# Squares on ScalarE, x loaded twice, a later weight schedule and turned PSUM banks in a hybrid decoder block

## The chip, the core and the metric

The kernel runs on one core of a Trainium2 chip. The metric is the device time of one execution in microseconds (us), the median over several runs; lower is better. Profiles are taken in one extra execution by the hardware profiler. TensorE appears there as PE (matmul) and PEld (weight load), VectorE as DVE, ScalarE as ACT, GpSimd as POOL, SyncE as SP; a name with q (SPq, ACTq) is the engine's instruction queue, on which DMAs are issued.

## The reference, cut to what matters

One decoder layer, 1024 tokens of width 1024, float32. x is normalised per token and modulated per channel, then multiplied by one wide input matrix:

```python
mod = c @ w_ada + b_ada
shift, scale, gate = jnp.split(mod, 3, axis=-1)
h = rmsnorm(x, norm_g) * (1.0 + scale) + shift      # mean of x*x over the 1024 channels of a token
proj = h @ w_in                                      # 1024 -> 6656 columns
q, k, v, g_attn, xr, g_rnn, m_attn, m_rnn = jnp.split(proj, SPLIT_POINTS, axis=-1)
q, k = partial_rope(q, positions), partial_rope(k, positions)
y_attn = sliding_window_attention_with_sinks(q, k, v, sinks) * silu(g_attn)
xr = causal_depthwise_conv(xr, conv_w, conv_b)
y_rnn = rg_lru(xr, ...) * silu(g_rnn)
merged = sigmoid(m_attn) * (y_attn @ w_attn_proj) + sigmoid(m_rnn) * (y_rnn @ w_rnn_proj)
out = rmsnorm(x + gate * (merged @ w_out), final_g)
```

## The kernel before, in words

All of h is kept transposed: channels on the 128 partitions, the 1024 tokens along the row, in eight tiles (kc = 0 to 7), each cut into two halves of 512 tokens (hf). Float32 accuracy is reached with two numbers of a shorter type for each factor: a high part (`hh`, `wh`, a copy into float32r on ACT) and the rest (`hl`, `wl`, a subtraction on DVE). Every product is three matmuls: high x high, rest x high, high x rest. The order of instructions on every engine is written out by hand (`manual_schedule`), so each engine runs its list strictly in the order of the program.

**The start.** SP asks for the eight tiles `xT` of x transposed, 512 KB each, first; then for the modulation weights `wada` (two tiles of 512.5 KB for each kc, by `load_ss`, six buffers) and for the first weights of `w_main` (256 KB halves, by `load_half`, six buffers `r`). `c_row` and `pk` (per-channel constants) are asked for on ACT's queue, `posr` and `invf` (for the rope angles) on POOL's. DVE works out the rope angles (`angles`, some 30 small instructions, up to L321). ACT squares each `xT` tile (L254), in four buffers; DVE adds pairs of squares (L256); TensorE sums over the channels with a column of ones, 8 groups of 128 tokens for each of the five sums (L250, `sums`), into PSUM bank `bk[2]`. DVE adds the five groups (L339), ACT takes the root (`root_of`), DVE the reciprocal, and TensorE spreads it over the partitions (L348, `spread`) into `bk[0]` and `bk[1]`. `modulate(kc, a)` is a DVE multiply-and-sum over a `wada` tile and a broadcast copy of c (`c_bc`, L237); it gives shift and scale of the 128 channels of kc. `norm` multiplies by the spread root (L353, L356), `high` makes `hh` on ACT straight from the normalised tile (L359), `affine` makes the full h in place on ACT (L363), `low` subtracts (L368).

Four column groups of 128 of `w_main` are multiplied while h is being made (`starts`, L170 by `mm_k`): for each kc 24 matmuls of 128x512. `starts[0]` and `starts[1]` (k) add up in `pmain` tiles, `starts[2]` (q, first part) in `bk[2:]`, `starts[3]` (q, second part) in `bk[:2]`. `cast_w`/`rest_w` split their weights: half 0 serves kc 0 to 3 and lies in four tiles `first`; half 1 serves kc 4 to 7 and lies in the five-buffer tags `wh`/`wl` (`slot()`).

**After the start.** TensorE goes on with the v product (`v_product`, L1383 to L1385, 96 matmuls for each half of the tokens), two products of the merge gate (`merge`, L170, 48 matmuls each), one small matmul into `bk[0]` (L1437), and then 22 pairs of column groups by a Strassen-like scheme (`Pair`, `run`, L597), seven products each. `place` gives pair i its banks: `b1 = bk[0]`, `b2 = bk[1 + par]`, `b3 = bk[3]` and, for one product at the very end, `bk[2 - par]`; par alternates from pair to pair. In the meantime DVE and ACT rotate q and k (`rope_a` with rotation, `rope_b` without), form the differences of h that the scheme needs (`differences`, `make_operands`) and split weights. Near the end of the pairs the attention is woven in: `open_attn` asks for its first tiles, `scores` is L1140, `values` L1212. Behind the last pair the products `rp` of the recurrent branch (L170, two PSUM tiles `rp0` and `rp1`, which take the places of `bk[0]`, `bk[1]` and of `bk[2]`, `bk[3]`) run between the attention's units. The last pair ends with two readings of its banks: `keep` (L646, ACT, copies `b2`) and `add` (L668, DVE, adds the fourth bank).

The line that chooses the banks:

```python
p.place(7 * i, i % 2, i == len(pairs) - 1, ...)
```

Of the kernel before, what the change touches and what calls it, by code (L numbers as in the profile page):

```python
# [22 lines left out]
P = 128  # L23
S = 1024
# [27 lines left out]
def tile_hybrid_block(ctx, tc, x, x_t, pk, rows, posr, posi, invf, c_row, w_ss, w_gate, w_main, w_v,  # L52
# [4 lines left out]
    def dma(dst, src, eng=nc.sync):  # L57
        dst, src = (a.bitcast(F32) if a.dtype == F32R else a for a in (dst, src))
        return eng.dma_start(dst, src)  # L59
# [96 lines left out]
    hx = h_ctx.enter_context(tc.tile_pool(name="hx", bufs=8))  # L156
    acc, r_bc = (hx.tile([P, S], F32, tag="X", name=n_) for n_ in ("acc", "r_bc"))
    xT = [xx.tile([P, S], F32, name=f"xT{kc}") if kc % 4 == 3 else
# [27 lines left out]
    with ExitStack() as st:  # L186
        sp = st.enter_context(tc.tile_pool(name="start", bufs=1, side="right"))
        first = [tuple(sp.tile([P, HALF], F32R, name=f"{n}0{i}") for n in ("wh", "wl"))
                 for i in range(4)]
        sqs = [acc, sp.tile([P, S], F32, name="sqa"), r_bc, sp.tile([P, S], F32, name="sqb")]  # L190
        c_row_t = sqs[3][0:1, :]
        posr_t = sp.tile([P, 64], I32, name="posr_t")
        invf_t = sp.tile([P, 1], F32, name="invf_t")
        dma(c_row_t, c_row, A)
        dma(pk_t[:], pk, A)
        dma(posr_t[:], posr, G)
        dma(invf_t[:], invf, G)

        wada, halfw = {}, {}

        def load_ss(kc):
            for a in range(2):
                wa_t = sp.tile([P, D + 1], F32, tag="wada", name="wada", bufs=6)
                dma(wa_t[:], w_ss[a * D + kc * P:a * D + (kc + 1) * P, :])
                wada[kc, a] = wa_t
# [3 lines left out]

        for kc in range(KC):  # L210
            dma(xT[kc][:], x_t[kc * P:(kc + 1) * P, :])
        load_ss(0)
        for i in range(4):
            load_wh(i, 0)
        load_ss(1)
        load_ss(2)
        for i in range(2):
            load_wh(i, 1)

        make_identity(nc, ident)  # L220
        one = sp.tile([P, P], F32, name="one")
        V.memset(one[:], 1.0)
        root = sp.tile([P, 1], F32, name="root")
        A.activation(root[:], one[:, 0:1], AF.Sqrt)
        c_bc = sp.tile([P, D + 1], F32, name="c_bc")
        V.memset(c_bc[:, D:], 1.0)
        for hf in range(2):
            T.matmul(bk[hf], one[0:1, :], c_row_t[:, SL[hf]], start=True, stop=True)
        for hf in range(2):
            A.copy(c_bc[:, SL[hf]], bk[hf])  # L230

        mods = sp.tile([P, 16], F32, name="mods")
        gsc = sp.tile([P, 8], F32, name="gsc")

# [12 lines left out]

        def sums(i, kc, js=range(8)):
            for j in js:
                T.matmul(bk[2][:, 8 * i + j:8 * i + j + 1], sqs[kc % 4][:, j * P:(j + 1) * P],  # L250
                         one[:, 0:1], start=True, stop=True)

        def square(kc):
            A.activation(sqs[kc % 4][:], xT[kc][:], AF.Square)  # L254
            if kc < 6 and kc % 2:
                V.tensor_tensor(out=sqs[kc % 4 - 1][:], in0=sqs[kc % 4 - 1][:],  # L256
                                in1=sqs[kc % 4][:], op=ALU.add)
                sums(kc // 2, kc - 1)

        trn = sp.tile([P, 2, 64], F32, name="trn")  # L260
        trf = trn[:].rearrange("p a t -> p (a t)")
# [60 lines left out]

        csn = sp.tile([P, 3, 64], F32, name="csn")

        def table():
# [7 lines left out]

        rr = tiny("rr", 8)
        groups = bk[2][:, 0:40].rearrange("p (g j) -> p j g", j=8)

        def root_of(hf):
            r1 = rr[:, 4 * hf:4 * hf + 4]
            V.tensor_reduce(out=r1, in_=groups[:, 4 * hf:4 * hf + 4, :], axis=AX.X, op=ALU.add)  # L339
            V.tensor_scalar(out=r1, in0=r1, scalar1=1.0 / D, scalar2=EPS, op0=ALU.mult,  # L340
                            op1=ALU.add)
            A.activation(r1, r1, AF.Sqrt)
# [30 lines left out]
        def cast_w(i, h):  # L373
            W0[i, h] = slot() if h else first[i]
            cast(W0[i, h], halfw[i, h], 0.125 if i > 1 else 1.0)
# [7 lines left out]

        angles()
        square(0)
        square(1)
        for kc in range(2, 6):
            square(kc)
        square(6)
        sums(3, 6)  # L390
        square(7)
        for hf in range(2):
            sums(4, 7, range(4 * hf, 4 * hf + 4))
        modulate(0, 0)
        root_of(0)
        root_of(1)
        spread(0)
        spread(1)
        cast_w(0, 0)
        cast_w(1, 0)  # L400
        modulate(0, 1)
        norm(0, 0)
        high(0, 0)
        rest_w(0, 0)
        norm(0, 1)
        high(0, 1)
# [16 lines left out]
        load_ss(3)  # L423
        for i in (2, 3):
            load_wh(i, 1)
        for kc in range(1, KC):
            norm(kc)
            for hf in range(2):
                high(kc, hf)
            affine(kc)  # L430
            if kc == 1:
                table()
            if kc + 1 < KC:
                for a in range(2):
                    modulate(kc + 1, a)
            if kc in (2, 3):
                for i in (0, 1) if kc == 2 else (2, 3):
                    cast_w(i, 1)
                    rest_w(i, 1)
            low(kc)  # L440
            if kc + 3 < KC:
                load_ss(kc + 3)
            if kc == 3:
                rv = [load_half(w_v[i // 2][:, SL[i % 2]]) for i in range(4)]
            if kc < 3:
                for terms in ("h", "l"):
# [990 lines left out]
    T.matmul(bk[0], hh[0][0][:, 0:P], hh[0][0], start=True, stop=True)  # L1437
# [45 lines left out]
    for u in range(32 + 3):  # L1483
# [286 lines left out]
```

## Time and profile before

| what | value |
|---|---|
| median of 3 runs | 961.26 us (961.08 to 964.26) |
| profiled execution: its time, its span | 960.87 us, 959.2 us |
| granted TensorE clock, mean over the span | 0.991 |
| PE busy | 924.6 us (96%) |
| DVE busy | 684.2 us (71%) |
| ACT busy | 535.1 us (56%) |
| bytes moved | 164.21 MB |

Rows of the order of time (the timeline) give start, duration, engine, line, operation, written tile, read tiles, and in brackets how long the engine had been idle before and what ended that. The view of waits gives total, number of times and the longest. The view of windows gives for each stretch of time the busy time of each engine, then the granted clock, the mean share of the DMA engines and GB/s. Lines are those of the kernel before unless the text says otherwise.

### The profile page before, as it was taken

What the parts mean: (1) busy time and instruction counts of PE and PEld (TensorE: products, weight loads), DVE (VectorE), ACT (ScalarE), POOL (GpSimd) and SP (SyncE); (2) the same over time, 40 slices, a digit from 0 to 9 for tenths busy, and PEclk for the clock granted to TensorE, in tenths of its full rate; (3) what the DMA queues carried; (4) which work ended last, traced back from release to release, by engine and by line L of the source; (5) the groups of instructions that cost most, each with busy time, mean ns of one, the idle gap of its engine ahead of it and who ended that gap; (6) DMA issues with size and microseconds to landing.
All of it is one profiled execution on the core that took longest, in us unless ns stands there. A gap on an engine that the chain in (4) does not pass through costs nothing.

```text
span 959.2 us, 12443 instructions
## 1 busy us (share of the span) xinstructions
PE 924.6 (96%) x4305; PEld 769.6 (80%) x4305; DVE 684.2 (71%) x1044; ACT 535.1 (56%) x1019; POOL 86.5 (9%) x148
## 2 busy tenths in 40 slices
PE   4989999999999999999999998899999999999997
PEld 3867988888788888888887887778888888888886
DVE  4596688889866984888498474869899846657422
ACT  3355365654565954885678783868888632222211
POOL 0011000000000000000000001334444400000000
PEclk9999999999999999999999999989999999999999
DMA  9462355967232443336045257969566266446311
GB/s 355 131 218 80 102 184 186 315 222 253 72 111 96 139 154 99 110 110 207 35 165 173 91 175 244 307 240 296 177 198 224 83 238 245 161 147 241 132 66 66
DMA packets 80916, 164.21 MB, mean 171 GB/s; under 512 B 12531, under 2 KB 28915, under 8 KB 80854
## 3 DMA queue, kind: packets, MB, share of 16 engines
q1 hardware_dynamic: 77300, 155.24, 47.7%
q0 software_dynamic: 2256, 6.03, 1.9%
q10 hardware_dynamic: 1298, 2.15, 0.6%
q8 instruction: 34, 0.56, 0.2%
q14 instruction: 28, 0.23, 0.1%
HBM read 114.01 MB, written 49.78 MB: 171 GB/s over the span
## 4 chain that ended last, share of the span: by engine, by line
PE 90%; DVE 4%; DMA 2%; ACT 2%; issue 1%; POOL 0%; SPq 0%; DVEq 0%; ACTq 0%; POOLq 0%
PE bk L597 41%; PE rp L170 14%; PE pmain L170 6%; PE rp L1633 5%; PE pgate L891 5%; PE pmain L1633 4%; PE bk L170 4%; PE s_ps L1140 3%; PE pv L1212 3%; PE bk L250 2%; PE pt L1178 1%; DMA qs<-q_d 1%; PE bk L1383 1%; PE bk L1384 1%; PE bk L1385 1%
## 5 line engine op out<-in xcount | busy, mean ns | idle before, releaser
L597 PE MATMUL bk<-nh,wl 128*128 128x512 f32 x352 | 138.0, 392 | 0.4 <-DVE wl L107 0.4
L597 PE MATMUL bk<-nh,wh 128*128 128x512 f32 x352 | 137.8, 392 | 0.0
L597 PE MATMUL bk<-nl,wh 128*128 128x512 f32 x352 | 137.6, 391 | 0.0
L107 DVE TENSOR_TENSOR wl<-r,wh 128x512 fp32r<-128x512 f32 x109 | 79.3, 732 | 24.1 <-ACT wh L101 24.1
L101 ACT CAST wh<-r 128x512 fp32r<-128x512 f32 x109 | 66.9, 618 | 46.1 <-PE bk L1385 12.7
L597 PEld LDWEIGHTS bk<-nh,wl 128*128 128x128 f32 x352 | 66.5, 189 | 15.2 <-DVE wl L107 1.4
L597 PEld LDWEIGHTS bk<-nh,wh 128*128 128x128 f32 x352 | 66.4, 189 | 13.9
L597 PEld LDWEIGHTS bk<-nl,wh 128*128 128x128 f32 x352 | 66.5, 189 | 13.7
L597 PE MATMUL bk<-hh,wh 128*128 128x512 f32 x176 | 68.6, 390 | 0.0
L597 PE MATMUL bk<-hh,wl 128*128 128x512 f32 x176 | 68.6, 390 | 0.0
L597 PE MATMUL bk<-hl,wh 128*128 128x512 f32 x176 | 68.5, 389 | 0.0
L107 DVE TENSOR_TENSOR wl<-ws,wh 128x512 fp32r<-128x512 f32 x76 | 51.8, 686 | 0.5 <-ACT wh L101 0.5
L1164 ACT ACTIVATE p<-p,small 128x129 f32<-128x129 f32 x128 | 50.1, 401 | 0.0
L101 ACT CAST wh<-ws 128x512 fp32r<-128x512 f32 x76 | 45.8, 614 | 2.3 <-DVE ws L619 1.1
L59 POOL DMA_DIRECT2D yh_d<-yh x1 | 0.6, 557 | 491.7 <-ACT yh L958 491.7
L1140 PE MATMUL s_ps<-ks,qs 128*128 128x256 f32 (+1 forms) x256 | 37.6, 289 | 3.2 <-DMA qs<-q_d 3.2
L597 PEld LDWEIGHTS bk<-hh,wh 128*128 128x128 f32 x176 | 33.0, 188 | 7.7 <-ACT wh L101 0.9
L1650 ACT ACTIVATE o<-xo 128x1024 f32<-128x1024 f32 (+2 forms) x10 | 8.9, 889 | 53.4 <-DVE xo L1649 53.4
L597 PEld LDWEIGHTS bk<-hl,wh 128*128 128x128 f32 x176 | 33.0, 188 | 6.9
L597 PEld LDWEIGHTS bk<-hh,wl 128*128 128x128 f32 x176 | 33.0, 188 | 6.7
L1140 PEld LDWEIGHTS s_ps<-ks,qs 128*128 128x128 f32 x256 | 32.4, 190 | 3.9 <-issue 3.6
L700 ACT ACTIVATE c<-bk 128x512 f32<-128x512 f32 x29 | 17.3, 597 | 31.0 <-PE bk L597 31.0
(361 smaller groups left out, 2327.0 us busy)
## 6 DMA issues: line engine op xcount, KB each, us to landing
r<-w_main SPq DMA_DIRECT2D x100, 256.0 KB, 4.1
wada<-w_ss SPq DMA_DIRECT2D x16, 512.5 KB, 4.8
qs<-q_d SPq DMA_DIRECT2D x16, 512.0 KB, 5.4
ks<-k_d SPq DMA_DIRECT2D x24, 192.0 KB, 3.5
xT<-x_t SPq DMA_DIRECT2D x8, 512.0 KB, 7.3
q_d<-rhi SPq DMA_DIRECT2D x16, 256.0 KB, 4.2
q_d<-rlo SPq DMA_DIRECT2D x16, 256.0 KB, 3.8
sma_d<-c SPq DMA_DIRECT2D x16, 256.0 KB, 2.8
```

What stands on the lines that cost most here:

```text
L101: A.copy(dst[0][:], src)
L107: V.tensor_tensor(out=dst[1][:], in0=src, in1=f32(dst[0][:]), op=ALU.subtract)
L170: mm = T.matmul(ps[hf], ww, xx[kc][hf], start=(kc == 0 and ww is w_h and xx is xh), stop=(kc == KC - 1 and xx is xl))
L250: T.matmul(bk[2][:, 8 * i + j:8 * i + j + 1], sqs[kc % 4][:, j * P:(j + 1) * P], one[:, 0:1], start=True, stop=True)
L597: W["pe"] = T.matmul(ps, ww[:, c], b[kc][xx_], start=(first and kc == 0 and i == 0), stop=(kc == 3 and i == 2), skip_group_check=not first)
L700: A.activation(t["t"], s(), AF.Tanh, scale=0.5)
L891: W["pe"] = T.matmul(ps[:, SL[hf]], ww[:, c0:c0 + P], xx_[:, SL[hf]], start=(ic == 0 and i == 0), stop=(ic == 1 and i == 2))
L1140: W["pe"] = T.matmul(o, qs[:, j, qc], ks[:, b, k0 + (0 if n else P):k0 + 256], start=(b == 0), stop=(b == 1))
L1164: A.activation(px[:, j, :], px[:, j, :], AF.Exp, bias=sm[:, 0, j:j + 1], accum_out=sm[:, 1, j:j + 1])
L1178: W["pe"] = T.transpose(pt[:, j, :], px[:, j, 0:P], ident[:])
L1212: W["pe"] = T.matmul(pv[:], b, m[:].rearrange("p j q -> p (j q)"), start=(i == 0), stop=(i == len(prods) - 1))
L1633: T.matmul(ps[:, sl], lhs[k][th][:, ts_], w[:, sl], start=(k == 0 and w is h_ and lhs is mh), stop=(k == KC - 1 and lhs is ml))
```

## The change

The sum of squares is now taken along token rows: x is loaded a second time, untransposed (eight tiles of 128 tokens), before everything else on SP's queue, and ACT squares each tile with a running sum (`accum_out`), giving eight columns of `rr`; TensorE's sums, DVE's additions and the four square buffers are gone. `mean` and `root_of` work on four columns at a time. The row tiles share the `wada` buffers, now seven; one of them lies in a tile `xlast`. `xT[kc]` is asked for behind the `wada` tiles of its kc. `posr` and `invf` move to ACT's queue, the copies of `c_bc` from ACT to DVE. In the loop over kc the affine tile comes first and `hh` is a plain copy of it. Half 0 of the start's weights now lies in `slot()`, half 1 in `first`; the v weights are split during kc = 5, 6 and 7 instead of behind the loop. The last four kc of the loop take the starts in the order 2, 3, 0, 1. ACT copies `starts[2]` out of its banks (`kept`) before the v product, which now begins in `bk[2:]`; the banks of `merge` are exchanged likewise, and `place` starts with the other parity. `open_attn` asks for the first k and q tiles ahead of the sinks. The tiles `nh` are laid out in another order, and the pool of the start is released tile by tile.

```diff
-    acc, r_bc = (hx.tile([P, S], F32, tag="X", name=n_) for n_ in ("acc", "r_bc"))
+    r_bc, xlast = (hx.tile([P, S], F32, tag="X", name=n_) for n_ in ("r_bc", "xlast"))
...
-        sp = st.enter_context(tc.tile_pool(name="start", bufs=1, side="right"))
+        sp = pool(st, "start", side="right")
...
+        c_row_t = r_bc[0:1, :]
         dma(c_row_t, c_row, A)
+        dma(posr_t[:], posr, A)
+        dma(invf_t[:], invf, A)
         dma(pk_t[:], pk, A)
-        dma(posr_t[:], posr, G)
-        dma(invf_t[:], invf, G)
...
-                wa_t = sp.tile([P, D + 1], F32, tag="wada", name="wada", bufs=6)
+                wa_t = sp.tile([P, D + 1], F32, tag="wada", name="wada", bufs=7)
...
-        for kc in range(KC):
+        def load_xt(kc):
             dma(xT[kc][:], x_t[kc * P:(kc + 1) * P, :])
-        load_ss(0)
-        for i in range(4):
-            load_wh(i, 0)
-        load_ss(1)
-        load_ss(2)
-        for i in range(2):
-            load_wh(i, 1)
+
+        def load_x0(i):
+            t = xlast if i == 6 else sp.tile([P, D + 1], F32, tag="wada", name="xt", bufs=7)
+            dma(t[:, :D], x[i * P:(i + 1) * P, :])
+            xt.append(t[:, :D])
+
+        for i in range(8):
+            load_x0(i)
...
-        for hf in range(2):
-            A.copy(c_bc[:, SL[hf]], bk[hf])
...
-        def sums(i, kc, js=range(8)):
-            for j in js:
-                T.matmul(bk[2][:, 8 * i + j:8 * i + j + 1], sqs[kc % 4][:, j * P:(j + 1) * P],
-                         one[:, 0:1], start=True, stop=True)
-
-        def square(kc):
-            A.activation(sqs[kc % 4][:], xT[kc][:], AF.Square)
-            if kc < 6 and kc % 2:
-                V.tensor_tensor(out=sqs[kc % 4 - 1][:], in0=sqs[kc % 4 - 1][:],
-                                in1=sqs[kc % 4][:], op=ALU.add)
-                sums(kc // 2, kc - 1)
+        def square(i):
+            junk = sp.tile([P, D], BF16, tag="junk", name="junk")
+            A.activation(junk[:], xt[i], AF.Square, accum_out=rr[:, i:i + 1])
...
-            W0[i, h] = slot() if h else first[i]
+            W0[i, h] = first[i] if h else slot()
...
         angles()
-        square(0)
-        square(1)
-        for kc in range(2, 6):
-            square(kc)
-        square(6)
-        sums(3, 6)
+        for hf in range(2):
+            V.tensor_copy(c_bc[:, SL[hf]], bk[hf])
+        for i in range(7):
+            square(i)
+            if i == 1:
+                load_ss(0)
+                load_xt(0)
+                for j in range(4):
+                    load_wh(j, 0)
+            if i == 3:
+                load_ss(1)
+                load_xt(1)
+        mean(0)
+        root_of(0)
         square(7)
-        for hf in range(2):
-            sums(4, 7, range(4 * hf, 4 * hf + 4))
+        load_ss(2)
+        load_xt(2)
+        for i in range(2):
+            load_wh(i, 1)
+        spread(0)
         modulate(0, 0)
-        root_of(0)
+        mean(1)
         root_of(1)
-        spread(0)
-        spread(1)
+        A.copy(r_bc[:, SL[0]], bk[0])
+        modulate(0, 1)
         cast_w(0, 0)
-        cast_w(1, 0)
-        modulate(0, 1)
         norm(0, 0)
         high(0, 0)
+        spread(1)
         rest_w(0, 0)
+        cast_w(1, 0)
         norm(0, 1)
         high(0, 1)
         rest_w(1, 0)
+        cast_w(2, 0)
+        A.copy(r_bc[:, SL[1]], bk[1])
+        rest_w(2, 0)
         affine(0)
-        modulate(1, 0)
-        cast_w(2, 0)
+        cast_w(3, 0)
         low(0)
-        for hf in range(2):
-            A.copy(r_bc[:, SL[hf]], bk[hf])
-        cast_w(3, 0)
-        rest_w(2, 0)
-        modulate(1, 1)
         rest_w(3, 0)
+        for a in range(2):
+            modulate(1, a)
...
             norm(kc)
+            affine(kc)
             for hf in range(2):
-                high(kc, hf)
-            affine(kc)
+                A.copy(hh[kc][hf], xT[kc][:, SL[hf]])
...
-                for i in (3, 2, 0, 1):
+                for i in (2, 3, 0, 1):
...
-        wv = [split(slot(), r) for r in rv]
+            if kc in (5, 6, 7):
+                for i in ((0,), (1,), (2, 3))[kc - 5]:
+                    wv.append(split(slot(), rv[i]))
...
-    nh = [hn.tile([P, S], F32R, name=f"nh{i}") for i in range(KC)]
+    nh = dict((i, hn.tile([P, S], F32R, name=f"nh{i}")) for i in (3, 7, 2, 6, 1, 5, 0, 4))
...
-            p.place(7 * i, i % 2, i == len(pairs) - 1,
+            p.place(7 * i, (i + len(pairs) + 1) % 2, i == len(pairs) - 1,
...
+        fill_sink = sink(0)
+        load_kq(0)
         dma(W["sink"][:], rows[0:1, 2048:2048 + NH].to_broadcast([P, NH]))
-        sink(0)
-        load_kq(0)
+        fill_sink()
...
+    kept = [blk(), blk()]
+    for hf in range(2):
+        A.copy(kept[hf], starts[2][1][hf])
     now(*[rope_b(lambda hf=hf: starts[3][1][hf], hf, q_d[0]) for hf in range(2)])
-    now(*[rope_a(lambda hf=hf: starts[2][1][hf], hf, q_d[0]) for hf in range(2)])
-    v_product(bk[:2], 0)
+    v_product(bk[2:], 0)
+    for hf in range(2):
+        now(rope_a(lambda: kept[hf], hf, q_d[0]))
...
-    v_product(bk[2:], 1)
-    v_store(bk[:2], 0)
+    v_product(bk[:2], 1)
+    v_store(bk[2:], 0)
...
-    merge(0, bk[:2])
-    v_store(bk[2:], 1)
+    merge(0, bk[2:])
+    v_store(bk[:2], 1)
...
-    merge_out(0, bk[:2])
+    merge_out(0, bk[2:])
...
-    merge(1, bk[2:])
-    merge_out(1, bk[2:])
+    merge(1, bk[:2])
+    merge_out(1, bk[:2])
     T.matmul(bk[0], hh[0][0][:, 0:P], hh[0][0], start=True, stop=True)
```

More of the change, by code (lines that the diff above doesn't have):

```diff
@@ L38 @@
 PAD_R = 480
+PAD_S = 544
 def _split_const(u):
@@ L186, in tile_hybrid_block @@
     with ExitStack() as st:
-        sp = st.enter_context(tc.tile_pool(name="start", bufs=1, side="right"))
+        sp = pool(st, "start", side="right")
         first = [tuple(sp.tile([P, HALF], F32R, name=f"{n}0{i}") for n in ("wh", "wl"))
                  for i in range(4)]
-        sqs = [acc, sp.tile([P, S], F32, name="sqa"), r_bc, sp.tile([P, S], F32, name="sqb")]
-        c_row_t = sqs[3][0:1, :]
+        one = sp.tile([P, P], F32, name="one")
+        c_bc = sp.tile([P, D + 1], F32, name="c_bc")
+        trn = sp.tile([P, 2, 64], F32, name="trn")
+        csn = sp.tile([P, 3, 64], F32, name="csn")
         posr_t = sp.tile([P, 64], I32, name="posr_t")
         invf_t = sp.tile([P, 1], F32, name="invf_t")
+        mods = sp.tile([P, 16], F32, name="mods")
+        gsc = sp.tile([P, 8], F32, name="gsc")
+        root = sp.tile([P, 1], F32, name="root")
+        rr = sp.tile([P, 8], F32, name="rr")
+        sp.tile([P, PAD_S // 4], F32, name="pad_s")
+        c_row_t = r_bc[0:1, :]
         dma(c_row_t, c_row, A)
+        dma(posr_t[:], posr, A)
+        dma(invf_t[:], invf, A)
         dma(pk_t[:], pk, A)
-        dma(posr_t[:], posr, G)
-        dma(invf_t[:], invf, G)
-        wada, halfw = {}, {}
+        xt, wada, halfw = [], {}, {}
         def load_ss(kc):
             for a in range(2):
-                wa_t = sp.tile([P, D + 1], F32, tag="wada", name="wada", bufs=6)
+                wa_t = sp.tile([P, D + 1], F32, tag="wada", name="wada", bufs=7)
                 dma(wa_t[:], w_ss[a * D + kc * P:a * D + (kc + 1) * P, :])
@@ L208, in load_wh @@
             halfw[i, h] = load_half(w_main[i][:, SL[h]])
-        for kc in range(KC):
+        def load_xt(kc):
             dma(xT[kc][:], x_t[kc * P:(kc + 1) * P, :])
-        load_ss(0)
-        for i in range(4):
-            load_wh(i, 0)
-        load_ss(1)
-        load_ss(2)
-        for i in range(2):
-            load_wh(i, 1)
+        def load_x0(i):
[4 more added lines that the diff above has]
+            load_x0(i)
         make_identity(nc, ident)
-        one = sp.tile([P, P], F32, name="one")
         V.memset(one[:], 1.0)
-        root = sp.tile([P, 1], F32, name="root")
         A.activation(root[:], one[:, 0:1], AF.Sqrt)
-        c_bc = sp.tile([P, D + 1], F32, name="c_bc")
         V.memset(c_bc[:, D:], 1.0)
@@ L228, in tile_hybrid_block @@
             T.matmul(bk[hf], one[0:1, :], c_row_t[:, SL[hf]], start=True, stop=True)
-        for hf in range(2):
-            A.copy(c_bc[:, SL[hf]], bk[hf])
-        mods = sp.tile([P, 16], F32, name="mods")
-        gsc = sp.tile([P, 8], F32, name="gsc")
         def modulate(kc, a):
@@ L246, in tiny @@
             return sp.tile([P, n], F32, name=name)
-        def sums(i, kc, js=range(8)):
-            for j in js:
-                T.matmul(bk[2][:, 8 * i + j:8 * i + j + 1], sqs[kc % 4][:, j * P:(j + 1) * P],
-                         one[:, 0:1], start=True, stop=True)
-        def square(kc):
-            A.activation(sqs[kc % 4][:], xT[kc][:], AF.Square)
-            if kc < 6 and kc % 2:
-                V.tensor_tensor(out=sqs[kc % 4 - 1][:], in0=sqs[kc % 4 - 1][:],
-                                in1=sqs[kc % 4][:], op=ALU.add)
-                sums(kc // 2, kc - 1)
-        trn = sp.tile([P, 2, 64], F32, name="trn")
+        def square(i):
+            junk = sp.tile([P, D], BF16, tag="junk", name="junk")
+            A.activation(junk[:], xt[i], AF.Square, accum_out=rr[:, i:i + 1])
         trf = trn[:].rearrange("p a t -> p (a t)")
@@ L321, in angles @@
             V.tensor_scalar(out=trf, in0=trf, scalar1=-3.1415925, scalar2=None, op0=ALU.max)
-        csn = sp.tile([P, 3, 64], F32, name="csn")
         def table():
@@ L332, in table, with mean @@
             dma(cs4_d, cs_d.unsqueeze(1).to_broadcast([24, 4, S]), G)
-        rr = tiny("rr", 8)
-        groups = bk[2][:, 0:40].rearrange("p (g j) -> p j g", j=8)
+        def mean(hf):
+            r1 = rr[:, 4 * hf:4 * hf + 4]
+            V.tensor_scalar(out=r1, in0=r1, scalar1=1.0 / D, scalar2=EPS, op0=ALU.mult,
+                            op1=ALU.add)
         def root_of(hf):
             r1 = rr[:, 4 * hf:4 * hf + 4]
-            V.tensor_reduce(out=r1, in_=groups[:, 4 * hf:4 * hf + 4, :], axis=AX.X, op=ALU.add)
-            V.tensor_scalar(out=r1, in0=r1, scalar1=1.0 / D, scalar2=EPS, op0=ALU.mult,
-                            op1=ALU.add)
             A.activation(r1, r1, AF.Sqrt)
@@ L423, in tile_hybrid_block @@
         load_ss(3)
+        load_xt(3)
         for i in (2, 3):
             load_wh(i, 1)
+        wv = []
         for kc in range(1, KC):
             norm(kc)
+            affine(kc)
             for hf in range(2):
-                high(kc, hf)
-            affine(kc)
+                A.copy(hh[kc][hf], xT[kc][:, SL[hf]])
             if kc == 1:
@@ L442, in tile_hybrid_block @@
                 load_ss(kc + 3)
+                load_xt(kc + 3)
             if kc == 3:
@@ L1127, in sink @@
         gs = slice(u // 8 * 4, u // 8 * 4 + 4)
-        G.tensor_copy(px[:, :, P:P + 1], W["sink"][:, gs].unsqueeze(2))
+        return lambda: G.tensor_copy(px[:, :, P:P + 1], W["sink"][:, gs].unsqueeze(2))
     def scores(u):
@@ L1507, in tile_hybrid_block @@
         if u + 1 < 32:
-            sink(u + 1)
+            sink(u + 1)()
         if 2 <= u < 34:
```

## The prediction

> **What bounds the kernel now.** I read the page's busy times and chain first, then TensorE's waits, then the order of time at each wait.
>
> ```profile
> PE 924.6 (96%) x4305; PEld 769.6 (80%) x4305; DVE 684.2 (71%) x1044; ACT 535.1 (56%) x1019; POOL 86.5 (9%) x148
> PE 90%; DVE 4%; DMA 2%; ACT 2%; issue 1%; POOL 0%; SPq 0%; DVEq 0%; ACTq 0%; POOLq 0%
> PE bk L250 <- DVE acc L256: 10.0, 1, 10.0
> PE rp L170 <- DVE u L668: 4.6, 1, 4.6
> PE s_ps L1140 <- DMA qs<-q_d: 3.2, 1, 3.2
> ```
>
> TensorE is the bound and hardly ever waits, so time is to be won only where it waits or does work that can go: before the first product, at hla (64.7 us), at qs and at L668. The start:
>
> ```profile
> 9.22 0.26 DVE L267 TENSOR_SCALAR ang<-posf,invf_t 128x64 f32<-128x64 f32 x1 [2.64 <-DMA invf_t<-invf]
> 15.68 0.23 DVE L321 TENSOR_SCALAR trn<-trn 128x128 f32<-128x128 f32 x1
> 20.70 1.06 ACT L254 ACTIVATE acc<-xT 128x1024 f32<-128x1024 f32 x1 [9.23 <-PE bk L250]
> 30.86 3.55 PE L250 MATMUL bk<-one,sqb 128*128 128x1 f32 x16
> 34.45 0.18 DVE L339 TENSOR_REDUCE rr<-bk 128x4 f32<-128x20 f32 x1 [9.34 <-PE bk L250]
> 35.43 3.75 PE L348 MATMUL bk<-ident,rr 128*128 128x128 f32 x16 [1.01 <-DVE rr L346]
> 39.10 0.79 PE L170 MATMUL pmain<-hha,wh 128*128 128x512 f32 x1
> 45.83 1.22 DVE L356 TENSOR_TENSOR xT<-xT,r_bc 128x1024 f32<-128x1024 f32 x1
> 64.69 0.79 PE L170 MATMUL bk<-hla,wh 128*128 128x512 f32 x1 [2.76 <-DVE hla L368]
> 91.92 0.62 PE L170 MATMUL pmain<-hh,wl 128*128 128x512 f32 x2
> 92.37 0.61 PE L170 MATMUL pmain<-hl,wh 128*128 128x512 f32 x2
> 93.67 0.39 PE L1383 MATMUL bk<-wh,hha 128*128 128x256 f32 x1 [0.68 <-DVE rlo L532]
> ```
>
> The angles occupy DVE to 15.9, the pair sums follow, and ACT stands 9.23 us, until TensorE has freed its square buffers. The last sums end at 34.4, the first product starts at 39.10. From there to 64.69 DVE sets the pace; then TensorE runs through to 92.8.
>
> **The start, part by part.** TensorE's 80 sum matmuls (17.1 to 34.4) and DVE's three pair sums go. Loads, and the rows by which DVE and ACT are costed:
>
> ```profile
> xT<-x_t SPq DMA_DIRECT2D x8, 512.0 KB, 7.3
> DMA to landing us min/median/max: 4.8/7.3/8.8
> pk_t<-pk ACTq DMA_DIRECT2D x1, 48.0 KB, 4.8
> 0.00:12.00 12.00, 3.75 (x4) 1.16 (x4) 2.81 (x16) 6.45 (x8) 1.94 (x8) 1.00 0.80 297
> 12.00:24.00 12.00, 6.91 (x32) 6.90 (x32) 6.96 (x21) 2.00 (x2) 0.00 (x0) 1.00 1.03 414
> L1650 ACT ACTIVATE o<-xo 128x1024 f32<-128x1024 f32 x7 | 7.4, 1061 | 45.9 <-DVE xo L1649 45.9
> 59.27 1.23 DVE L237 SCALAR_TENSOR_TENSOR jk<-wada,c_bc 128x1025 bf16<-128x1025 f32 x1
> 67.96 1.24 ACT L363 ACTIVATE xT<-xT,mods,gsc 128x1024 f32<-128x1024 f32 x1
> 69.24 1.29 DVE L368 TENSOR_TENSOR hl<-xT,hh 128x512 fp32r<-128x512 f32 x2 [0.25 <-ACT xT L363]
> ```
>
> The x rows take the place, size and row length of the old xT loads on SP: first landing 5.6 (0.8 + 4.8), last about 13.5. By 12 us 3.56 MB had landed, then 414 GB/s. Eight x tiles, two wada, xT0 and the first weight half are 6.1 MB with the small loads, so wada(0) lands at 14.8 and 16.1, xT0 at 17.4, the weight at 18.1. SP's queue now waits for squares 0 to 5 ahead of wada(0) to wada(2), and all weights stand behind it; these squares end by 12.5, and the transfers asked for still fill the DMA engines to 13.5, so I cost that at nothing. Without that cover the weights would come later one for one.
>
> A square with its running sum costs 1.06 (L1650, same shape), between nothing and 0.2 more for reading the sum; I take 1.1. Eight, with a root between the seventh and the last, end at 16.3. On DVE the angles need 6.7 us (9.22 to 15.9) from the landing of invf. That is now on ACT's queue; the bounds are 6.2 (pk there) and 9.2 (POOL before). I take 6.2, since pk is nearest in queue and time. So angles to 13.1, two c_bc copies (1.3, as the two 128x512 of L368) to 14.4, mean, root and reciprocal to 15.2. Half of the spreads (3.75 / 2) gives 17.1. Two modulates (1.3 each) end at 18.3, norm follows at 18.4 to 19.1, hh at 19.9, the second spread holds TensorE to 21.2: the first product comes at 21.2 instead of 39.1. DVE's list then goes: norm of the other half 22.0, two rests with one wait for a cast 24.2, affine wait, low 26.5, rest 27.1, two modulates 29.8. norm(1) starts at 29.9 instead of 45.83: 15.9 earlier.
>
> From norm(1) to hla of kc 3 DVE took 18.86. The new order, affine (1.24) then two copies (0.6 each, as L646 below), replaces two `high` (1.5) and affine on ACT, so low waits less: three waits like the 0.25 at 69.24, with casts behind two of them, about 1.0. hh itself comes 1 us later, which TensorE has to spare there. All these loads end well ahead of DVE at 414 GB/s (wada(3) at 31 against 36 when needed). From hla TensorE needs the same 28.1. The starts end at 75.9, 16.9 earlier. The v weights are split in kc 5 to 7, where DVE and ACT have room, and `kept` needs only starts[2], the first of the last four, so the 0.68 and the handover go: 0.8. Together **-17.7** at the v product. The wait at kc 3 stays; the next thing late is hla again.
>
> **The banks.** The small matmul L1437 writes bk[0], which after the change ACT still has to read for the second merge:
>
> ```profile
> 138.82 0.39 PE L1437 MATMUL bk<-hha 128*128 128x512 f32 x1
> 139.54 0.50 PE L597 MATMUL bk<-hha,wl 128*128 128x512 f32 x1
> 139.74 1.09 ACT L1423 ACTIVATE c<-bk 128x512 f32<-128x512 f32 x2
> 142.18 0.39 PE L597 MATMUL bk<-nh,wh 128*128 128x512 f32 x1
> ```
>
> Half of 1.09 after 139.74 is 140.3; then L1437 (0.23) and a first product of 12 x 0.2275 (the two matmuls from 91.92 to 92.37 took 0.45) end at 143.3 instead of 142.18: **+1.1**. In the old banks no such wait existed. ACT's list there hangs on the v product's end, so it moves with TensorE.
>
> At the other end the gain lies:
>
> ```profile
> 619.78 1.20 PE L1140 MATMUL s_ps<-ks,qs 128*128 128x256 f32 x8
> 619.92 0.59 ACT L646 COPY u<-bk 128x512 f32<-128x512 f32 x1 [0.87 <-DVE c L657]
> 624.83 0.68 DVE L668 TENSOR_TENSOR u<-u,bk 128x512 f32<-128x512 f32 x1
> 625.57 1.22 PE L170 MATMUL rp<-hha,wh 128*128 128x512 f32 x2 [4.59 <-DVE u L668]
> 630.00 1.05 PE L170 MATMUL rp<-hla,wh 128*128 128x512 f32 x2
> 64.00:68.50 4.50, 3.81 (x10) 2.83 (x11) 4.46 (x7) 2.06 (x3) 0.00 (x0) 0.62 0.69 256
> 625.50:631.00 5.50, 5.43 (x13) 4.28 (x14) 0.79 (x3) 0.63 (x1) 0.00 (x0) 0.50 0.38 143
> ```
>
> With 22 pairs the last had par 1, so L668 read bk[1], under rp0. Turned, bk[1] is b2, free when L646 ends at 620.5; L668 then holds bk[2], under rp1, which is first written one unit later (about 626.2, L668 over at 625.5). rp0 starts at 621.0: 4.6. And its 12 matmuls ran at a granted clock of 0.50, 5.29 instead of 2.73: 2.56 more. **-7.1.** DVE, which idled behind that stall, now has to follow without a pause; its list in a unit is about 4.5 us against TensorE's 5.2, so I give nothing back.
>
> ```profile
> 581.37 0.33 SPq L59 DMA_DIRECT2D sink<-rows  x1
> 581.93 1.54 SPq L59 DMA_DIRECT2D ks<-k_d  x2
> ```
>
> k and q are asked for one place earlier, 0.56: **-0.6** of the 3.2 wait. POOL's sink copy and the v loads behind it start some 3 us later; values read them some 20 us on.
>
> Sum: -17.7 + 1.1 - 7.1 - 0.6 = -24.3. The profiled execution took 960.87 (0.4 below the median), so **936.6 us**.
>
> [...] A pause of 2.76 lowered the clock to 0.62 and one of 4.59 to 0.50, while one of 0.68 (93.67) did not; the new pause at L1437 is 1.5. I take no loss; the other bound is 8 matmuls at 0.43 (5.29 / 12) instead of 0.23, 1.6 us. [...] Against the move of invf speaks that 4.8 and 7.1 us were measured on two queues under the same flood of xT. [...]
>
> **The rivals.**
> 1. invf no sooner: angles to 15.9, everything behind them 2.8 later: 939.4. For it: no row shows so small a load on ACT's queue. Chance 0.10.
> 2. The clock falls at L1437: 938.2. Chance 0.10.
> 3. The start gains only half: 4 MB more in front, SP's queue waiting for ACT and DVE. At the 225 GB/s that the start reached from 48 to 60 us the first weight would land near 29.6 instead of 18.1; with part of that hidden, 8 to 10 lost: 945. Against it: 414 GB/s with eight loads outstanding. Chance 0.13.
>
> ```profile
> 48.00:60.00 12.00, 11.77 (x48) 8.83 (x48) 10.88 (x19) 7.85 (x10) 3.23 (x5) 1.00 0.75 225
> ```
>
> 4. The wait at rp stays, because DVE or a load is late instead: only its 7.1 is lost, 943.7. For it: L668 is no earlier, and DMA was at its limit just before. Chance 0.10.
> 5. Slower: the turned banks make the first product of each pair wait for an eviction. 22 pairs decide from 1.3 us each ((24.3 + 4.8) / 22); at 1.5 it is 969.6. Against it: within a pair the exchange of bk[1] and bk[2] is symmetrical, and only the first and last pair see fixed neighbours. Chance 0.04.
> 6. The start does not shorten, since the DVE list sets it all along, and DVE eats the rp gain: 960 or so. Chance 0.03.
>
> **The numbers.** My forecast holds 0.50, range 931 to 941 alone (the start +-4, the clock at kc 3 -1.6). With rivals 1 to 4 the range is 930.5 to 946.5. Rivals 5 and 6 lie outside. Half a per cent, 4.8 us, is about what a measurement can tell; faster 0.93, the same 0.03, slower 0.04.
>
> **What would show it.** First product near 21, norm(1) near 30, v product near 76; squares without a wait for TensorE and the last ending near 16; invf near 6; one wait of TensorE for L1423 of about 1.5; none for L668; the qs wait near 2.6. Wrong it would be if the first wada landed after 20, if TensorE waited for `low` at several kc after kc 3, or if products of pairs waited for ACT.

## The result and the profile after

The changed kernel takes 937.68 us (median; 936.42 to 938.5) beside 962.18 for the kernel before, a ratio of 0.9742 (95% interval 0.972 to 0.9764). The profiled execution took 938.5 us, the highest of its times, with a span of 936.4. In the new kernel `mm_k` is L171, the products L602, the small matmul L1447, `keep` L651, `add` L673, the scores L1146.

The busy times of the changed kernel (TensorE 21.0 us less than the 924.6 before), then its start in order of time:

```profile
PE 903.6 (97%) x4225; PEld 749.2 (80%) x4225; DVE 680.8 (73%) x1041; ACT 533.5 (57%) x1027; POOL 86.9 (9%) x146
```

```profile
9.28 0.25 DVE L260 TENSOR_SCALAR ang<-posf,invf_t 128x64 f32<-128x64 f32 x1 [3.06 <-DMA invf_t<-invf]
17.27 0.20 ACT L332 ACTIVATE rr<-rr 128x4 f32<-128x4 f32 x1 [2.12 <-DVE rr L327]
23.16 0.77 PE L171 MATMUL pmain<-hha,wh 128*128 128x512 f32 x1
31.67 1.22 DVE L346 TENSOR_TENSOR xT<-xT,r_bc 128x1024 f32<-128x1024 f32 x1
34.87 0.49 PE L171 MATMUL pmain<-hha,wh 128*128 128x512 f32 x1 [2.57 <-ACT hha L432]
49.46 0.50 PE L171 MATMUL bk<-hla,wh 128*128 128x512 f32 x1 [0.59 <-DVE hla L358]
76.26 0.28 PE L1389 MATMUL bk<-wh,hha 128*128 128x256 f32 x1
```

The v product starts 17.4 us earlier (76.26 for 93.67). invf landed as late as before, 9.28. The pause at kc 3 shrank from 2.76 to 0.59, and a pause of 2.57 stands at kc 1. The windows (busy time of PE, PEld, DVE, ACT and POOL, then the granted clock, the share of the DMA engines, GB/s) show where the slow clock went:

```profile
33.00:40.00 7.00, 5.10 (x14) 3.88 (x15) 6.89 (x11) 5.99 (x8) 2.82 (x4) 0.76 1.03 417
48.00:52.00 4.00, 3.31 (x13) 2.17 (x12) 4.00 (x6) 0.83 (x1) 0.00 (x0) 1.00 1.04 418
```

It is at kc 1, where DVE, busy 6.89 of 7.00 us, sets the pace, and no longer at kc 3, from where TensorE sets it.

The places that decide later, of the changed kernel:

```profile
122.66 0.50 PE L1447 MATMUL bk<-hha 128*128 128x512 f32 x1 [1.41 <-ACT c L1433]
125.74 0.39 PE L602 MATMUL bk<-nh,wh 128*128 128x512 f32 x1
575.88 1.11 PE L1146 MATMUL s_ps<-ks,qs 128*128 128x256 f32 x8
579.08 0.58 ACT L705 ACTIVATE c<-bk 128x512 f32<-128x512 f32 x1
583.92 0.33 ACTq L60 DMA_DIRECT2D smr_d<-c  x1
584.29 0.62 ACT L102 CAST wh<-ws 128x512 fp32r<-128x512 f32 x1 [4.63 <-DMA hla<-yl_d]
586.22 1.21 PE L1146 MATMUL s_ps<-ks,qs 128*128 128x256 f32 x8 [2.33 <-DVE p L1160]
603.12 1.20 PE L1146 MATMUL s_ps<-ks,qs 128*128 128x256 f32 x8
604.60 0.74 PE L171 MATMUL rp<-hha,wh 128*128 128x512 f32 x2 [0.27 <-ACT u L651]
608.76 1.20 PE L1146 MATMUL s_ps<-ks,qs 128*128 128x256 f32 x8
842.36 1.07 PE L1643 MATMUL rp<-wo,hha 128*128 128x512 f32 x4
```

and the rows of the kernel before that answer to 575.88, 608.76 and 842.36:

```profile
597.37 1.10 PE L1140 MATMUL s_ps<-ks,qs 128*128 128x256 f32 x8
632.30 1.20 PE L1140 MATMUL s_ps<-ks,qs 128*128 128x256 f32 x8
864.78 1.07 PE L1633 MATMUL rp<-wo,hha 128*128 128x512 f32 x4
```

Read as differences: -17.4 at the v product, -16.4 at 125.74 (142.18 before), -21.5 at the second scores, -16.7 at 603.12 (619.78 before), -23.5 at 608.76, -22.4 at the final product. The last product ahead of the attention is 16.5 us earlier than before. So the attention's opening won 5.0 us and gave 4.8 back in the next 27 us, rp won 6.9, and 1.1 was given back behind it. The two profiled executions lie 22.4 us apart (960.87 and 938.5), as the final product does; the medians lie 24.5 apart.

### The profile page after: what moved, and what is told of

Read it like the earlier page. It is cut to its first block, busy times and chain, and to the rows that moved or that the text cites. A ratio compares the mean times of both kernels' runs of the same rounds, so it can differ in the third digit from the quotient of the medians.

```text
span 936.4 us, 12299 instructions
## 1 busy us (share of the span) xinstructions
PE 903.6 (97%) x4225; PEld 749.2 (80%) x4225; DVE 680.8 (73%) x1041; ACT 533.5 (57%) x1027; POOL 86.9 (9%) x146
## 4 chain that ended last, share of the span: by engine, by line
PE 80%; DVE 4%; DMA 2%; ACT 1%; issue 1%; POOL 0%; ACTq 0%; SPq 0%; DVEq 0%
PE bk L602 42%; PE rp L171 13%; PE rp L1643 5%; PE pmain L171 5%; PE pgate L896 5%; PE pmain L1643 4%; PE s_ps L1146 2%; PE pv L1218 2%; PE pt L1184 1%; DMA ks<-k_d 1%; DMA r<-w_rp 1%; DVE wl L108 1%; DVE plc L1195 1%; DVE small L1165 0%; DVE p L1160 0%
## 5 line engine op out<-in xcount | busy, mean ns | idle before, releaser
L602 PE MATMUL bk<-nh,wl 128*128 128x512 f32 x352 | 137.3, 390 | 0.4 <-DVE wl L108 0.4
L602 PE MATMUL bk<-nh,wh 128*128 128x512 f32 x352 | 137.1, 389 | 0.0
L602 PE MATMUL bk<-nl,wh 128*128 128x512 f32 x352 | 137.0, 389 | 0.0
L602 PEld LDWEIGHTS bk<-nh,wl 128*128 128x128 f32 x352 | 66.1, 188 | 14.9 <-DVE wl L108 1.4
L602 PEld LDWEIGHTS bk<-nl,wh 128*128 128x128 f32 x352 | 66.1, 188 | 13.7
L602 PEld LDWEIGHTS bk<-nh,wh 128*128 128x128 f32 x352 | 66.1, 188 | 13.7
L602 PE MATMUL bk<-hh,wh 128*128 128x512 f32 x176 | 68.6, 390 | 0.0
L602 PE MATMUL bk<-hh,wl 128*128 128x512 f32 x176 | 68.6, 390 | 0.0
L602 PE MATMUL bk<-hl,wh 128*128 128x512 f32 x176 | 68.5, 389 | 0.0
L1146 PE MATMUL s_ps<-ks,qs 128*128 128x256 f32 (+1 forms) x256 | 37.6, 289 | 2.4 <-DVE p L1160 2.3
L602 PEld LDWEIGHTS bk<-hh,wh 128*128 128x128 f32 x176 | 33.0, 188 | 7.6 <-ACT wh L102 0.9
L602 PEld LDWEIGHTS bk<-hh,wl 128*128 128x128 f32 x176 | 33.0, 188 | 7.0 <-DVE wl L108 0.3
L602 PEld LDWEIGHTS bk<-hl,wh 128*128 128x128 f32 x176 | 33.0, 188 | 6.9
L1146 PEld LDWEIGHTS s_ps<-ks,qs 128*128 128x128 f32 x256 | 32.5, 190 | 3.2 <-DVE p L1160 2.9
```

What stands on the lines that cost most here:

```text
L602: W["pe"] = T.matmul(ps, ww[:, c], b[kc][xx_], start=(first and kc == 0 and i == 0), stop=(kc == 3 and i == 2), skip_group_check=not first)
L1146: W["pe"] = T.matmul(o, qs[:, j, qc], ks[:, b, k0 + (0 if n else P):k0 + 256], start=(b == 0), stop=(b == 1))
```

## The experiments

The diffs are against the changed kernel, but for `turn_alone`. Differences of stages are read from one profiled execution each. Where one time is given, the kernel was timed once; four times of the changed kernel alone lie from 936.42 to 938.5, so a single time that is 1 or 2 us lower shows little by itself.

**The parts alone.** `turn_alone` is the kernel before with only the parity turned; `start_alone` is the changed kernel with the parity and the order in `open_attn` undone; `old_banks` undoes the parity only.

```diff
-            p.place(7 * i, (i + len(pairs) + 1) % 2, i == len(pairs) - 1,
+            p.place(7 * i, i % 2, i == len(pairs) - 1,
```

Expected of turn_alone: 

> The kernel before with the turned banks alone. If the banks alone make the gain at rp: no wait there, 12 rp matmuls in 2.75 instead of 5.3 us, 6.9 less; the first pair's first product now writes bk[2], which ScalarE reads until about 140.3 for the second merge, 0.8 more; time about 955 (six less than the 960.6 to 962.2 of before). If the gain needs the earlier start, the time stays at 961. It also tells whether the wait for qs of 3.23 us belongs to the order of the loads (then 3.2 again, with the slow clock behind it) or to the execution shown (then about 1, as with the sink first in the changed kernel).

Expected of start_alone: 

> The changed kernel without the turned banks and without the earlier k and q: the start alone. If the parts add up, the v product comes at 76.3 and the time is 962.2 - 17.4 + about 1 to 1.5 for the waits at the small matmul and the first product = 946. If the start is in part given back later, it is above 948; if the opening's 2.2 us (573.5 against 575.6 with the same order of loads) come from the start too, it is near 943.5.

Expected of old_banks: 

> The changed kernel, with the pairs' banks as before (parity i % 2). If the turned banks took away the wait at rp, TensorE waits again some 4.6 us for the add of the last pair, the 12 rp matmuls take 5.3 instead of 2.75 us, and the time is about 938.5 + 7.0 = 945.5; the first attention scores and everything ahead of them stay within 0.7 us of the changed kernel. If the wait went because everything now comes earlier (rival), rp stays without a wait and the time at 938.5.

`turn_alone` took 954.48 us, one time beside 962.31 for the kernel before:

```profile
140.20 0.50 PE L597 MATMUL bk<-hha,wh 128*128 128x512 f32 x1 [1.18 <-ACT c L1423]
592.02 1.08 PE L1140 MATMUL s_ps<-ks,qs 128*128 128x128 f32 x8 [2.33 <-DMA qs<-q_d]
620.79 0.63 PE L170 MATMUL rp<-hha,wh 128*128 128x512 f32 x2
624.81 1.19 PE L1140 MATMUL s_ps<-ks,qs 128*128 128x256 f32 x8
```

No wait at rp, 7.5 us won there (624.81 for 632.30), and a new wait of 1.18 at the first product, as expected. That wait did not even reach the attention: the scores stand at 592.02 as before (592.06), because q landed no sooner, and the wait for it shrank from 3.23 to 2.33.

`start_alone` took 945.44 (before 962.31), as its first theory had it. The two parts sum to -24.7, the whole change to -24.5; the order in `open_attn` is in neither of them, so in the time it shows as nothing. In `start_alone` the first scores waited 2.36 us for q, and TensorE's clock fell behind that wait (the matmuls from 577.23 to 581.50 lie 0.43 us apart, those up to 572.25, ahead of the wait, 0.23).

`old_banks` took 947.15 us, 8.65 above the profiled execution of the changed kernel where 7.0 was expected:

```profile
586.26 1.21 PE L1146 MATMUL s_ps<-ks,qs 128*128 128x256 f32 x8 [2.56 <-DVE p L1160]
605.05 1.19 PE L1146 MATMUL s_ps<-ks,qs 128*128 128x256 f32 x8
610.27 1.22 PE L171 MATMUL rp<-hha,wh 128*128 128x512 f32 x2 [4.03 <-DVE u L673]
616.87 1.19 PE L1146 MATMUL s_ps<-ks,qs 128*128 128x256 f32 x8
```

The wait for the add is back, so the earlier start alone would not have removed it. From one scores to the next 11.82 us pass for 5.64 in the changed kernel: 6.2 us belong to the banks. The scores at 605.05 are 1.9 later on their own: 0.7 is there by 598.45 (597.78 in the changed kernel), as a second idle stretch of ACT lasts 3.14 instead of 2.52 us (below), and the rest comes between there and 605.05.

**The small matmul.** Into a bank that ACT has long read:

```diff
-    T.matmul(bk[0], hh[0][0][:, 0:P], hh[0][0], start=True, stop=True)
+    T.matmul(bk[2], hh[0][0][:, 0:P], hh[0][0], start=True, stop=True)
```

> The changed kernel, with the small matmul in bk[2], which ScalarE has read long before. If the wait of 1.41 us is the read of bk[0], it goes, the first product starts 1.0 us earlier (near 122.0 instead of 123.0), and the time is about 937.5. If DVE's operands are late there too, the wait only changes its name, and nothing moves.

It took 936.45 us, which is within the spread of the changed kernel. In the trace the wait is gone and the first product starts 1.5 us earlier (121.50 for 123.00); 0.25 of that is lost between the next two matmuls, the first scores come 1.1 us earlier:

```profile
121.27 0.39 PE L1447 MATMUL bk<-hha 128*128 128x512 f32 x1
121.50 0.39 PE L602 MATMUL bk<-hha,wh 128*128 128x512 f32 x1
```

**invf first.** posr and invf asked for on SP ahead of x (in the program the two new lines stand ahead of the load of `c_row`):

```diff
-        dma(posr_t[:], posr, A)
-        dma(invf_t[:], invf, A)
+        dma(posr_t[:], posr)
+        dma(invf_t[:], invf)
```

> The changed kernel, with posr and invf asked for by SP ahead of the x rows. If the late landing of invf (9.2 us) and the angles behind it set the start, the angles end near 10.5 instead of 15.9; then ScalarE's seventh square (about 15.9, as x comes two issues later) releases the first root instead of DVE: root near 16.0 instead of 17.27, first product near 22 instead of 23.16, norm(1) near 30.4 instead of 31.67, time about 936.4. Rival: the loads behind them set the start; then the first wada or weight is waited for, norm(1) stays near 31.7 and the time at 937.7.

It took 937.94 us: no gain. Timeline, then windows of TensorE (its busy time, granted clock, DMA share, GB/s):

```profile
3.48 0.25 DVE L260 TENSOR_SCALAR ang<-posf,invf_t 128x64 f32<-128x64 f32 x1 [0.68 <-DMA invf_t<-invf]
30.20 1.22 DVE L346 TENSOR_TENSOR xT<-xT,r_bc 128x1024 f32<-128x1024 f32 x1
33.40 0.50 PE L171 MATMUL pmain<-hha,wh 128*128 128x512 f32 x1 [1.93 <-ACT hha L432]
47.98 0.50 PE L171 MATMUL bk<-hla,wh 128*128 128x512 f32 x1 [1.50 <-DVE hla L358]
76.41 0.28 PE L1389 MATMUL bk<-wh,hha 128*128 128x256 f32 x1
```

```profile
48.00:50.00 2.00, 1.90 (x5) 0.74 1.04 411
50.00:52.00 2.00, 2.00 (x6) 0.50 1.04 421
52.00:54.00 2.00, 2.00 (x10) 0.91 0.95 379
```

The theory held as far as it went: norm(1) 1.5 us earlier, hla of kc 3 too. Then all of it went, in a place that neither theory named. Behind the pause at kc 1, here 1.93, the clock stayed up (1.00 from 34 to 42, where the changed kernel has 0.79); so TensorE was early at kc 3, waited there 1.50, and now the clock fell where TensorE sets the pace: 2 x (0.26 + 0.50 + 0.09) = 1.7 us.

**The old order on ACT** for kc 1 to 7:

```diff
             norm(kc)
-            affine(kc)
             for hf in range(2):
-                A.copy(hh[kc][hf], xT[kc][:, SL[hf]])
+                high(kc, hf)
+            affine(kc)
```

> The changed kernel, with the old order of ScalarE's work for k rows 1 to 7 (two activations to hh, then the affine, instead of the affine and two copies). If that order made the 1.07 us between norm(1) and hla of kc 3, they come back (18.86 instead of 17.79). Two theories of the clock: if the shorter pause at kc 3 (0.6 instead of 2.76) kept the clock up, the pause comes back near 2 us, the granted clock falls to about 0.6 there, and hla to the v product takes 28 to 29 instead of 26.8: time about 940 to 941. If the clock was held by something else (the pause of 2.57 moved to kc 1), hla to the v product stays at 26.8 and the time is about 938.8.

It took 942.85 us, more than either theory had. Timeline, then windows:

```profile
32.24 1.22 DVE L346 TENSOR_TENSOR xT<-xT,r_bc 128x1024 f32<-128x1024 f32 x1
51.09 0.80 PE L171 MATMUL bk<-hla,wh 128*128 128x512 f32 x1 [2.75 <-DVE hla L358]
80.38 0.28 PE L1389 MATMUL bk<-wh,hha 128*128 128x256 f32 x1
```

```profile
52.00:54.00 2.00, 2.00 (x6) 0.50 0.96 382
54.00:56.00 2.00, 2.00 (x6) 0.50 0.23 88
```

From norm(1) to hla 18.85 us (before 18.86), and from hla to the v product 29.3 for 26.8. So the order brought the 1.07 us on DVE, and 2.5 more by the clock at kc 3. (The v product is 4.1 later; 0.57 of that is a later invf in this execution.)

**The pause at kc 3 taken away**, on top of invf first (the other branch of this `if`, which takes the four starts one after the other, serves kc 3 to 7, five rows and not the last four):

```diff
-            if kc < 3:
+            if kc < 4:
                 for terms in ("h", "l"):
```

> invf_first, and at k row 3 TensorE does the products with hh for all four weights ahead of those with hl, as at rows 0 to 2. Alone, the earlier invf won 1.5 us up to kc 3 and lost it there: a pause of 1.50 us lowered the clock to 0.50 for 3.4 us. If that is the cause, the pause goes, the clock stays at 1.00 from 46 to 56 us, DVE's hl of row 4 sets the pace next (53.5), and the v product comes near 74.3 instead of 76.3 to 76.4: time about 935.7. If the v product is set by something else (v weights, ScalarE), it stays near 76.3 and the time at 937.7.

933.88 us (ratio to before 0.9716, 0.9694 to 0.9739). TensorE waits nowhere at kc 3, and the windows from 46 to 60 us all have the clock at 1.00:

```profile
50.00:52.00 2.00, 2.00 (x9) 1.00 1.04 422
73.84 0.28 PE L1389 MATMUL bk<-wh,hha 128*128 128x256 f32 x1
```

The v product comes 2.4 us earlier than in the changed kernel. That is the first experiment in which the start became shorter still. The medians differ by 3.8 us; the rest goes with ACT's idle stretch in the attention, which is 1.76 instead of 4.63 us in this profile, and with TensorE's wait of 2.33 us at the scores, which is gone. Why that stretch became shorter was not tried.

**ACT's stand in the attention.** Between 579.7 and 583.9 ACT does nothing; its next instruction is the issue of the store smr_d, at 583.92. The profile puts the end of that idle time down to the load hla, asked for on SP at 575.95 and landed 7.9 us later, at 583.9; the DMA share is 0.83 from 575 to 580 and 1.03 from 580 to 585. Why the issue of the store waits for that load is not shown. The chain of the changed kernel at that place has such a hold twice: SP asks for r at 586.64, 0.02 us after the load ks has landed, and ACT issues its next store at 593.55, 0.07 us after that r has landed:

```profile
577.37 9.25 DMA ks<-k_d
586.62 0.02 issue
586.64 6.84 DMA r<-w_rp
...
593.50 0.02 ACTq L60
...
593.98 0.07 ACT ob L1227
```

Two edits: the store on SP, or the old order of sink and k, q. `store` also puts the issue off to the end of the attention's unit, so the first edit changes the place of the store as well as its engine.

```diff
-                        dma(dst[j][:, SL[th]], t["t"], A if "att" in W else nc.sync)
+                        store(dst[j][:, SL[th]], t["t"])
```

> The changed kernel, with the stores of the tanh gates in attention issued by SP instead of ScalarE. Theory: ScalarE's two idle stretches of 4.63 and 2.52 us (580 to 594) are its own queue standing at a transfer that may not be issued until an older one has landed; then they go, TensorE's wait of 2.33 at the scores near 586 and the 0.7 near 594 go, and up to 4.8 us are won: 934 to 936. Rival: the loads are late because the DMA engines are full; then ScalarE or TensorE waits as long for the loads themselves, and the time stays at 938 to 939.

```diff
-        fill_sink = sink(0)
-        load_kq(0)
         dma(W["sink"][:], rows[0:1, 2048:2048 + NH].to_broadcast([P, NH]))
-        fill_sink()
+        sink(0)()
+        load_kq(0)
         load_kq(1)
```

> The changed kernel, with the sink asked for ahead of k and q, as before. If the place of the k and q loads made the gain of 5.0 us at the second scores, the wait for q comes back (about 3.2 us, then a slow clock for 1.6), second scores at about 380 us after the first scores of before's place, that is near 581 instead of 575.9. What then happens behind it tells the second thing: if ScalarE's 4.6 us stand at the transfer that it issues is only due to the earlier k and q, it goes too and the time is about 938.5; if the two are independent, the time is about 943.

`store_sp` took 933.5 us (one time), 4.2 less than the changed kernel, against 3.7 to 1.7 expected; the scores that had waited 2.33 us wait no more and come 3.1 earlier (0.5 of it from an earlier start in this execution):

```profile
583.14 1.19 PE L1146 MATMUL s_ps<-ks,qs 128*128 128x256 f32 x8
```

`sink_first` took 935.39 us. ACT's 4.63 us were gone, and with them 1.4 of the 5.0 us that the opening had won (577.25 for 575.88):

```profile
573.53 1.08 PE L1145 MATMUL s_ps<-ks,qs 128*128 128x128 f32 x8 [1.06 <-DMA qs<-q_d]
577.25 1.12 PE L1145 MATMUL s_ps<-ks,qs 128*128 128x256 f32 x8
```

Here q was waited for 1.06 us where 3.2 was expected, and the clock stayed up (matmuls 0.23 us apart from 574.97 on). As it looked faster than the changed kernel, it was timed again:

> sink_first once more, timed, beside the same before. Its profile ended 3.1 us earlier than the changed kernel's (first final product at 839.3 against 842.4). If that holds, 934.6 to 935.4 and a ratio near 0.9715; if it was that execution, 937 to 938 and 0.9742.

937.18 us (ratio 0.9752, 0.9728 to 0.9775): not to be told from the changed kernel. In this profile the wait for q was 1.82, the clock fell behind it (matmuls 0.43 us apart from 575.56 to 578.55), and 3.5 of the 5.0 us were gone:

```profile
574.08 1.08 PE L1145 MATMUL s_ps<-ks,qs 128*128 128x128 f32 x8 [1.82 <-DMA qs<-q_d]
579.39 1.11 PE L1145 MATMUL s_ps<-ks,qs 128*128 128x256 f32 x8
```

So the earlier k and q win at the opening (wait and clock; 1.4 and 3.5 us by these two profiles), and, as the times are alike, lose about as much at ACT. All six profiles with k and q first and the store on ACT show ACT standing for hla, 1.76 to 4.86 us; none of the five with the sink first and the store on ACT does. In `sink_first` ACT comes to the store at 581.0 instead of 579.7, hla was asked for at 574.93 instead of 575.95, and the store is issued at 581.05, without a wait.

**Together.** `all4` is split3_invf with the small matmul in `bk[2]` and the store on SP; `all5` is all4 with the sink first.

> split3_invf, the small matmul in bk[2], and the stores of the tanh gates on SP. If the four are independent: 937.7 - 2.0 - 1.0 - 4.9 = 929.8. If the attention's opening absorbs what comes earlier (its DMA engines are full), only the stores count there: 932 to 933.

> all4 with the sink asked for ahead of k and q, as before. If the loss behind the earlier k and q was ScalarE's stand at the transfer, which is gone here, the earlier k and q are now worth their 1.3 us at the opening: about 931. If they cost something by themselves (fuller DMA engines), this one is faster than all4, 927 to 929.

`all4` took 931.4 us (ratio 0.9685, 0.9663 to 0.9708), the fastest here and faster than the changed kernel, whose interval lies above; `all5` 933.8 (0.9713, 0.9691 to 0.9735). all4 came between its two theories: small_bank's 1.1 is there (first scores 568.64 for split3_invf's 569.88), but that leaves some 1.4 us for the store, not 4.9; in split3_invf the stand was only 1.76. With the stand gone, the order with k and q first is 2.4 us faster than the other (the times of the two do not overlap), which neither edit shows alone. Of that 1.1 us stand at the scores (572.32 for 573.41); the rest comes later, where `all5` waits 2.1 us for yl and yh.

## Why the prediction held, point by point

The start and the banks made the gain, as was said, and each does so alone. That the sum came so close is in part luck: inside the start two errors cancel, and so do two at the attention's opening. In the profiled executions the terms are -17.4, +1.0, -0.2, -6.9 and +1.1, together -22.4 where -24.3 was forecast.

- **The start, -17.7; measured -17.4, by two errors that cancel.** The step that failed is "I take 6.2" for invf. It landed 7.4 us after its issue on ACT's queue, DVE began with it at 9.28, and its angles, c_bc, mean and root followed: first product 23.16 instead of 21.2, norm(1) 31.67 instead of 29.9. That is rival 1: the angles' first instruction, which waits for invf, starts at 9.22 with invf on POOL's queue, at 9.28 on ACT's, and at 3.48 when it was asked for ahead of x. Of the 2.8 us that rival 1 put on it, 1.8 show at norm(1); at the v product 0.3 is left of them, for the next reason. The last square, expected to end near 16, ended at 18.5, as it stands behind the root on ACT. The other edits of the start were not undone one by one; that the sums' going made the 17.4 us is read from the rows.
- **"The wait at kc 3 stays" failed too, in the other direction.** The -1.0 on DVE was exact (17.79 for 18.86 from norm(1) to hla). But the wait nearly went, and the slow clock behind it with it (1.00 from 48 to 52): 26.8 us from hla to the v product where the sum had 28.1 and no wait for rlo. The prediction had both numbers (2.76 us and a clock of 0.62) in a row and treated them as fixed; high_twice shows 2.5 us on them. The wait shrank by 2.2 us: 1.07 is DVE's, and the other 1.1 is TensorE's own lateness. It comes to this wait 17.20 us after norm(1) (48.87) instead of 16.10 (61.93 before, 48.34 in high_twice), held up above all by the slow clock at kc 1 (0.76 from 33 to 40): in invf_first, where the clock stays up there (1.00 from 34 to 42), it comes 16.28 us after norm(1) and waits 1.50. The prediction saw that hh would come 1 us later, "which TensorE has to spare there", but not that the clock would fall behind that pause and make TensorE late enough to fill most of the wait at kc 3.
- **L1447, +1.1; measured +1.0**, the clock did not fall behind its 1.41 us (1.00 from 122 to 127; rival 2 did not come), and small_bank gives it back.
- **The opening, -0.6; measured -5.0 and then +4.8.** Two mis-sized things, a net of -0.2. That the wait for q would go, and the 1.6 us of slow clock behind it (0.50 from 594 to 596 before), was not seen; nor that ACT would then stand 4.63 us behind hla. How much of the 5.0 belongs to the order of the loads differs from one execution to the next: with the old order the second scores come 1.4 and 3.5 us later in the two of sink_first, and 6.0 in start_alone (581.90). The prediction counted who waits for the loads, but not that a store on ACT could stand until one of them has landed.
- **rp, -7.1; measured -6.9**, and -7.5 by the banks alone. "I give nothing back" missed 1.1 us behind it, which turn_alone gives back likewise (from -7.5 at the scores to -6.4 at the final product, 858.37 for 864.78). What takes it was not tried.
- **Rivals 3, 4, 5 and 6 did not come**: no gain was lost to the loads (411 to 418 GB/s from 33 to 52 us), the wait at rp is 0.27, and no pair waited (-16.4 before the pairs, and -16.5 at the last product ahead of the attention).
- **Two sums do not come out of their own terms.** 6.2 and 6.7 give 12.9 for the end of the angles, not 13.1. Rival 3's first weight at 29.6 does not follow from 3.56 MB by 12 us and 225 GB/s behind it, which give 23.3 for the 6.1 MB. Neither moves the forecast by more than 0.2.

## What to carry to other kernels

In these runs the slow clock behind a pause of TensorE cost time where TensorE sets the pace, 1.7 us at kc 3 in invf_first and 2.5 in high_twice, and none where DVE does: from norm(1) to hla it is 17.79 us with a clock of 0.76 at kc 1 and 17.78 in invf_first with 1.00. Making the work ahead of it faster can move the pause from a covered place to an open one and lose the whole gain, as invf_first did; so look which engine is busy around each slow-clock stretch and put independent matmuls there. When loads are moved, look up for each store that a computing engine issues what ends the idle time ahead of it: here ACT stood still, with all its arithmetic, 1.76 to 4.86 us behind a load that it has nothing to do with. And when parts are judged by one profile, time them: in two executions of one kernel the wait for q differed by 0.8 us, and the scores behind it, as the clock fell in one of them, by 2.1 us.

## What the runs showed of the hardware

The length of a pause does not decide alone whether the clock falls. It fell behind pauses of 2.76 us (the kernel before at kc 3, 0.62 from 64 to 68.5), 2.57 (the changed kernel at kc 1, 0.76 from 33 to 40), 2.36 (start_alone at q), 1.82 (sink_first_5 at q) and 1.50 (invf_first at kc 3, 0.50 from 50 to 52), and not behind 1.93 (invf_first at kc 1, 1.00 from 34 to 42), 1.41 (the changed kernel at L1447, 1.00 from 122 to 127) and 1.06 (sink_first at q). Where no clock is given, it is read from the 128x512 matmuls: in invf_first they lie 0.43 us apart from 50 to 52, at a clock of 0.50, and 0.23 from 54 to 56, at 1.00. Nor is there a limit between these lengths: behind a wait of 2.33 us the clock fell in turn_alone (592.02; matmuls 0.43 us apart from 593.54) and stayed at 1.00 in the changed kernel (586.22; from 586 to 590), and behind 2.56 in old_banks (586.26) the matmuls lie 0.23 us apart from 587.99 on. In invf_first the slow matmuls, from 48.92 to 52.28, last 3.4 us. What in the rows ahead of a pause decides is left open.
